# An MLP with its up and down projections apart, f kept on DRAM, and Strassen's seven block products in most of the down projection (Trainium2, one core)

## The chip, the core and the metric

The kernel runs on one core of a Trainium2 chip. The metric is the device time of one execution in microseconds, as the median of several runs; before the change it is 2465.88 us. A profile of one execution shows where the time goes on TensorE (PE, with its weight loads as PEld), VectorE (DVE), ScalarE (ACT), GpSimd (POOL) and the queue that issues DMAs (SP).

## What is computed

A trunk of two layers on 1024 tokens of width 1024 with 16 learned tokens ahead of them: differential attention, then a gated short convolution, each followed by an MLP with a squared ReLU. All in float32. The MLP is what the change concerns:

```python
def _sqrelu_mlp(h, w_up, w_down):          # w_up [1024, 4096], w_down [4096, 1024]
    a = jax.nn.relu(jnp.einsum('bld,df->blf', h, w_up))
    return jnp.einsum('blf,fd->bld', a * a, w_down)
```

The MLP's input is an RMSNorm of the residual stream, and its output is normed and added to the stream; layer 0's goes on into the convolution's three projections, layer 1's is the kernel's output.

## The kernel before

Activations stay transposed, channels on the 128 partitions and tokens along the columns. Every float32 product runs as three float32r passes: an operand is split into a part rounded to float32r (hi) and the remainder (lo), and hi·hi, hi·lo and lo·hi add up in PSUM (`product`, L166 to 174). Layer 0 works on T1 = 1026 columns (two learned tokens are still needed by the convolution), cut in three of 342; layer 1 on 1024, cut in two of 512.

Weights come as tiles of 128 x 1024 in the order of their use (`load_weights`, L122): SP loads 512 KB (L132), ScalarE casts hi (L143), VectorE subtracts lo (L144). Two pools, `wp` and `wx`, give two raw tiles and four pairs of hi and lo, so the next tiles are loaded and split ahead.

`mlp` (L406) goes through the 4096 f channels in 8 blocks of 4 tiles of 128. For a block it first does the up projection of each f tile over the 8 chunks of the input (24 matmuls per column chunk): VectorE takes the ReLU times the norm's scale out of PSUM (L424), ScalarE squares (L425), VectorE casts and subtracts (L426, L427) into `fh` and `fl`, which stay in SBUF. Then four weight tiles of the down projection, each for 256 output channels: 4 f tiles by 3 passes, 12 matmuls per half and column chunk. The result is copied into the accumulator `acc` in the first block (L450) and added to it in the others (L452). In the last block the squares for the following norm are summed on GpSimd (L198), and the norm is made where the columns are whole: `norm_step` (L354) in layer 0, `last_step` (L338) at the end of layer 1.

```python
for group in [[0, 1, 2, 3]] if last else [[0], [1], [2], [3]]:
...
    product(ps, w, lambda k, c: fh[k][:, c[0] : c[0] + c[1]],
            lambda k, c: fl[k][:, c[0] : c[0] + c[1]], half * FB * P, range(FB), cols)
```

PSUM has eight banks, of which seven go round for products. The order of the instructions on each engine is found by a scheduler from the program's dependences, except in stretches that fix it by hand (the attention's TensorE, the end of layer 1). `later`, `spent` and `settle` (L318 to 336) put the steps of a norm where enough products have been traced to cover them. After layer 0's MLP the convolution starts with a joint stage of four weight tiles, c and u of two channel groups (L552).

Of the kernel before, what the change touches and what calls it, by code (L numbers as in the profile page):

```python
# [23 lines left out]
P = 128  # L24
# [5 lines left out]
LEAD = META - 2  # L30
# [4 lines left out]
NB = FF // (FB * P)  # L35
# [3 lines left out]
CONV_ORDER = [0, 1, 3, 4, 2, 5] + list(range(6, 3 * KC))  # L39
REACH = T0 - P  # L40
BANKS = {"mm": 2, "s": 3, "t": 2, "o": 1}
E_BUFS = 3
EARLY = 3  # rows of the output projection begun within the attention
# the startup: steps of products between others, parts of the sums of squares, columns, banks of the first products
# [7 lines left out]
# engines and lags as the attention's order takes them  # L52
# [10 lines left out]
# the last layer's end: columns, squares summed on the tensor engine, and where each step goes  # L63
# [16 lines left out]
def trunk(ctx: ExitStack, tc: tile.TileContext, xt, wall, gains, lam_p, subln, convw, out):  # L80
# [7 lines left out]
    psp = ctx.enter_context(tc.tile_pool(name="psp", bufs=2, space=PSUM))  # L88
    drp = ctx.enter_context(tc.tile_pool(name="drp", bufs=1, space=DRAM))

    # one table serves every function used
# [15 lines left out]

    def big_tile(half, name, dtype=F32):
        return big.tile([P, 4, T0], dtype, tag=f"big{half}", name=f"{name}{half}")

    def late_tile(dtype):
        t = cst.tile([P, 2 * EARLY * P], dtype, tag="late", name="late" if dtype == F32R else "rs")
        return t if dtype == F32 else t.rearrange("p (a b) -> p a b", a=2)
# [8 lines left out]
    def load_weights(eng=None, raw=None, spare=None, early=None):  # L122
        """The next tile; gives what splits it. Of an early one, the last chunk's columns go to tiles of their own."""
# [29 lines left out]
    count = [0]  # L153

    def bank(tag, name):
        count[0] += 1
        return psp.tile([P, 512], F32, tag=tag, name=f"{name}_{count[0]}", bufs=BANKS[tag])

    ROUND = ["mm", "s", "t", "mm", "s", "t", "mm"]
    turn = [0]  # L160

    def any_bank(name):
        turn[0] += 1
        return bank(ROUND[turn[0] % len(ROUND)], name)

    def product(ps, w, hi, lo, w0, ks, cols):  # L166
        """ps += W^T x over the contraction chunks ks; W's chunk k starts at column w0 + k * P."""
        wh, wl = w
        n, last = 0, 3 * len(ks) - 1
        for j, k in enumerate(ks):  # L170
            a, b = w0 + j * P, w0 + (j + 1) * P
            for lhs, rhs in ((wh, hi), (wh, lo), (wl, hi)):
                nc.tensor.matmul(ps, lhs[:, a:b], rhs(k, cols), start=n == 0, stop=n == last)  # L173
                n += 1

    def rsqrt_mean(tp, ps, dst, n, dim):
        """dst = (-ps / dim + eps) ** -0.5, with a Newton step on what the tables give."""
# [7 lines left out]
    def total(sss, n):  # L185
        """minus the sum over the partitions of all of sss"""
        ps = bank("o", "sum")[:, :n]
# [12 lines left out]
    # ======== layer 0: differential attention ========  # L200
# [3 lines left out]
    HL = hpool.tile([P, KC, T0], F32R, name="HL")  # L204
# [8 lines left out]
    with pool("att") as att:  # L213
        with pool("xin", side="right") as xin, tc.manual_schedule(engines={ET.PE, ET.Activation, ET.DVE, ET.Pool}):
# [30 lines left out]
            def raw(z, cs):  # L245
                """not scaled yet by the norm: what these columns' products give is"""
# [60 lines left out]
    sp = ctx.enter_context(pool("sp", 3))  # L307
    wpools.append(ctx.enter_context(pool("wx", 2)))
# [4 lines left out]
    # ======== the rest ========  # L313
    # A step that closes a norm waits on other engines, so it is traced where that many us of products lie before it.
# [18 lines left out]
    def settle(step, cols):  # L333
        """what cols of the coming stage need of the steps up to this one"""
# [3 lines left out]
    def last_step(tp, m, sss, cols, res, res_out):  # L338
        """res_out <- res + rmsnorm(m) where m is gained already"""
# [14 lines left out]
    def norm_step(tp, layer, which, m, mss, cols, res_in, res_out, nxt, H, L, ssn, wait):  # L354
        """m <- res + rmsnorm(m), stored; then m * gain split into H and L, and its scale into ssn."""
# [6 lines left out]
        def add():  # L362
            rs = mss[:, s]
            rsqrt_mean(tp, total([rs], n), rs, n, D)
            for c4 in range(0, KC, 4):
                cs = slice(c4, c4 + 4)
                st = tp.tile([P, 4, n], F32, tag="st", name=f"st_{count[0]}_{c4}", bufs=2)
                nc.sync.dma_start(st, res_in(cs, s))
                for c in range(c4, c4 + 4):
                    mc, hc, gn = row(m, c, s), row(H, c, s), gain(nxt[0], nxt[1], c)  # L370
                    nc.vector.scalar_tensor_tensor(mc, mc, gain(layer, which, c), rs, ALU.mult, ALU.mult)
                    nc.vector.tensor_add(mc, mc, st[:, c - c4])
                    nc.scalar.activation(hc, mc, AF.Copy, scale=gn)
                    nc.vector.scalar_tensor_tensor(row(L, c, s), mc, gn, hc.bitcast(F32), ALU.mult, ALU.subtract)  # L374
                    add_square(tp, ssn[:, s], mc, c == 0, n, tag="sqn")
                nc.sync.dma_start(res_out(cs, s), m[c4 // 4][:, :, s])
# [29 lines left out]
    def mlp(tp, fp, hi, lo, rs, target, head, chunks, tail, after, final=False):  # L406
        """after(chunk, sum, its squares' sum) when a chunk is whole; target() once what came before is closed."""
        for b in range(NB):
            fh, fl = [], []
            for i in range(FB):  # L410
                fh.append(fp.tile([P, T1], F32R, tag="fh", name=f"fh_{b}_{i}", bufs=FB))
                fl.append(fp.tile([P, T1], F32R, tag="fl", name=f"fl_{b}_{i}", bufs=FB))
            for group in [list(range(FB))] if b == 0 else [[i] for i in range(FB)]:
                ws = [weights() for _ in group]
                for cols in head if b == 0 else chunks:
                    c0, n = cols
                    s = slice(c0, c0 + n)
                    for i, w in zip(group, ws):
                        ps = any_bank("up")[:, :n]
                        settle(0, cols)  # L420
                        product(ps, w, hi, lo, 0, range(KC), cols)
                        settle(1, cols)
                        r = fp.tile([P, n], F32, tag="r", name=f"r_{count[0]}", bufs=2)
                        nc.vector.scalar_tensor_tensor(r, ps, 0.0, rs[:, s], ALU.max, ALU.mult)  # L424
                        nc.scalar.activation(r, r, AF.Square)  # L425
                        nc.vector.tensor_copy(fh[i][:, s], r)  # L426
                        nc.vector.tensor_sub(fl[i][:, s], r, fh[i][:, s].bitcast(F32))  # L427
                        spent(3 * KC, n)
            last = b == NB - 1
            sqs, steps, scales, manual = [], [], [], ExitStack()  # L430
            if final and last:
                for c in range(0, KC, 2):
                    nc.sync.dma_start(YL[:, c : c + 2].bitcast(F32), res_dram[2][:, c : c + 2, :SEQ])
            if b == 0:
                acc, ass = target()
            for group in [[0, 1, 2, 3]] if last else [[0], [1], [2], [3]]:
                ws = [weights() for _ in group]
                for cols in tail if last else chunks:
                    if final and last and cols == tail[-1]:
                        manual.enter_context(tc.manual_schedule(engines=MANUAL))  # L440
                    c0, n = cols
                    s = slice(c0, c0 + n)
                    for gi, w in zip(group, ws):
                        for half in range(2):
                            mi = 2 * gi + half
                            ps, am = any_bank("dn")[:, :n], row(acc, mi, s)
                            product(ps, w, lambda k, c: fh[k][:, c[0] : c[0] + c[1]],
                                    lambda k, c: fl[k][:, c[0] : c[0] + c[1]], half * FB * P, range(FB), cols)
                            if b == 0:
                                nc.scalar.copy(am, ps)  # L450
                            else:
                                nc.vector.tensor_add(am, am, ps)  # L452
# [657 lines left out]
```

## Time and profile before

| what | value |
| --- | --- |
| median of 3 runs | 2465.88 us (2465.83 to 2465.95) |
| span of the profiled execution | 2461.8 us |
| around the span | 4.1 us |
| TensorE busy | 2405.5 us, 98% |
| VectorE, ScalarE, GpSimd busy | 1293.5, 868.1, 287.8 us |
| moved by DMA | 164.17 MB, 67 GB/s |

The span runs from the first to the last instruction. Busy shares are means over the whole span; the rows further down are read by stage.

### The profile page before, as it was taken

To read this page: it belongs to the slowest core of one execution; us is meant where nothing else is said; L and a number is where in the kernel's file an instruction comes from. 1 tells how busy PE (TensorE), PEld (TensorE's weight loads), DVE (VectorE), ACT (ScalarE), POOL (GpSimd) and SP (SyncE) were. 2 spreads that over 40 slices of the span, in tenths; PEclk is the share of its full clock that TensorE was granted. 3 is DMA by queue.
4 is the path that set the end of the run, shared out by engine and by line. 5 is a ranking of instruction groups with operands and counts; after the bars stand their busy time and mean duration, and the time that the engine had idled before them with its cause. 6 is when DMAs were issued, how large, how long until landed. Compare 5 with 4: busy or idle time off the path is not lost.

```text
span 2461.8 us, 34993 instructions
## 1 busy us (share of the span) xinstructions
PE 2405.5 (98%) x14186; PEld 2261.5 (92%) x14186; DVE 1293.5 (53%) x2559; ACT 868.1 (35%) x1725; POOL 287.8 (12%) x246
## 2 busy tenths in 40 slices
PE   8999999999999999999999999999999999999997
PEld 7899999999899999999999999999888888888887
DVE  7887777755823443443446934424823433433346
ACT  7777777655521111111114422224521111111125
POOL 3211211105200000000004200004200000000006
PEclk9999999999999999999999999999999999999998
DMA  4212222533511111111113411123411111111122
GB/s 133 65 53 61 61 62 68 137 106 92 140 52 44 50 45 44 52 44 52 44 52 81 117 47 43 52 66 79 122 52 43 52 43 52 43 52 43 52 70 102
DMA packets 77553, 164.17 MB, mean 67 GB/s; under 512 B 7248, under 2 KB 51664, under 8 KB 77392
## 3 DMA queue, kind: packets, MB, share of 16 engines
q1 hardware_dynamic: 77392, 161.94, 22.6%
q8 instruction: 111, 1.82, 0.3%
q14 instruction: 50, 0.41, 0.1%
HBM read 129.25 MB, written 24.15 MB: 62 GB/s over the span
## 4 chain that ended last, share of the span: by engine, by line
PE 83%; DVE 10%; DMA 2%; ACT 2%; issue 1%; SPq 0%; DVEq 0%; ACTq 0%
PE dn L173 27%; PE up L173 27%; PE mo L173 4%; PE bg L173 4%; PE ug L173 3%; PE cg L173 3%; PE po L1022 2%; DVE HL L374 1%; PE tr L983 1%; PE s L936 1%; PE s L937 1%; DMA w_raw<-in_wall 1%; PE v L689 1%; PE v L690 1%; PE v L691 1%
## 5 line engine op out<-in xcount | busy, mean ns | idle before, releaser
L143 ACT CAST w_hi<-w_raw 128x1024 fp32r<-128x1024 f32 (+2 forms) x191 | 199.2, 1043 | 792.7 <-PE dn L173 495.2
L173 PE MATMUL dn<-fh,w_hi 128*128 128x342 f32 (+2 forms) x1344 | 458.7, 341 | 0.5 <-DVE acc L452 0.5
L173 PE MATMUL dn<-fl,w_hi 128*128 128x342 f32 (+2 forms) x1344 | 458.1, 341 | 0.0
L173 PE MATMUL dn<-fh,w_lo 128*128 128x342 f32 (+2 forms) x1344 | 457.0, 340 | 0.0
L144 DVE TENSOR_TENSOR w_lo<-w_raw,w_hi 128x1024 fp32r<-128x1024 f32 (+1 forms) x167 | 206.3, 1235 | 228.3 <-ACT w_hi L143 228.2
L173 PEld LDWEIGHTS dn<-fh,w_hi 128*128 128x128 f32 x1344 | 253.1, 188 | 20.8 <-DVE acc L452 0.7
L173 PEld LDWEIGHTS dn<-fl,w_hi 128*128 128x128 f32 x1344 | 253.2, 188 | 19.6
L173 PEld LDWEIGHTS dn<-fh,w_lo 128*128 128x128 f32 x1344 | 252.9, 188 | 19.8
L173 PE MATMUL up<-HL,w_hi 128*128 128x342 f32 x768 | 246.1, 321 | 2.0 <-DVE HL L374 2.0
L173 PE MATMUL up<-HH,w_hi 128*128 128x342 f32 x768 | 245.4, 320 | 0.0
L173 PE MATMUL up<-HH,w_lo 128*128 128x342 f32 x768 | 244.9, 319 | 0.0
L424 DVE SCALAR_TENSOR_TENSOR r<-up,ssn 128x342 f32<-128x342 f32 (+2 forms) x164 | 93.8, 574 | 286.6 <-PE up L173 286.1
L425 ACT ACTIVATE r<-r 128x342 f32<-128x342 f32 (+2 forms) x164 | 87.8, 538 | 350.7 <-DVE r L424 350.5
L173 PE MATMUL up<-YL,w_hi 128*128 128x512 f32 (+2 forms) x544 | 209.1, 385 | 0.6 <-DVE YL L374 0.6
L198 POOL TENSOR_TENSOR ass<-ass,sq 128x256 f32<-128x256 f32 (+1 forms) x47 | 44.4, 944 | 1330.0 <-ACT sq L197 1329.6
L452 DVE TENSOR_TENSOR acc<-acc,dn 128x512 f32<-128x512 f32 (+1 forms) x128 | 78.7, 619 | 175.7 <-PE dn L173 175.5
L173 PEld LDWEIGHTS up<-HL,w_hi 128*128 128x128 f32 x768 | 144.7, 188 | 3.3 <-DVE HL L374 2.8
L173 PEld LDWEIGHTS up<-HH,w_lo 128*128 128x128 f32 x768 | 144.6, 188 | 0.3
L173 PEld LDWEIGHTS up<-HH,w_hi 128*128 128x128 f32 x768 | 144.8, 189 | 0.1
L173 PEld LDWEIGHTS up<-YL,w_hi 128*128 128x128 f32 x544 | 102.7, 189 | 21.4 <-DVE YL L374 1.2
L946 ACT ACTIVATE E<-E,mn 16x16 f32<-16x16 f32 (+5 forms) x144 | 105.2, 731 | 21.8 <-DVE mn L941 21.5
L173 PE MATMUL up<-YHa,w_hi 128*128 128x512 f32 (+2 forms) x272 | 104.3, 384 | 2.4 <-DVE r L424 2.4
(296 smaller groups left out, 5370.6 us busy)
## 6 DMA issues: line engine op xcount, KB each, us to landing
w_raw<-in_wall SPq DMA_DIRECT2D x189, 512.0 KB, 3.5
st<-res_dram SPq DMA_DIRECT2D x10, 684.0 KB, 9.6
st<-in_xt SPq DMA_DIRECT2D x6, 684.0 KB, 8.6
YL<-res_dram SPq DMA_DIRECT2D x4, 1024.0 KB, 9.4
HL<-on_dram SPq DMA_DIRECT2D x3, 1026.0 KB, 8.4
HH<-on_dram SPq DMA_DIRECT2D x3, 1026.0 KB, 11.0
out<-acc SPq DMA_DIRECT2D x12, 256.0 KB, 2.2
klb<-klb SPq DMA_DIRECT2D x32, 87.0 KB, 2.1
```

Of the source, the lines that this page charges most:

```text
L143: nc.scalar.copy(hi_part, raw[:, cols])
L144: (eng or nc.vector).tensor_sub(lo_part, raw[:, cols], hi_part.bitcast(F32))
L173: nc.tensor.matmul(ps, lhs[:, a:b], rhs(k, cols), start=n == 0, stop=n == last)
L198: (eng or nc.gpsimd).tensor_add(ss, ss, sq)
L374: nc.vector.scalar_tensor_tensor(row(L, c, s), mc, gn, hc.bitcast(F32), ALU.mult, ALU.subtract)
L424: nc.vector.scalar_tensor_tensor(r, ps, 0.0, rs[:, s], ALU.max, ALU.mult)
L425: nc.scalar.activation(r, r, AF.Square)
L452: nc.vector.tensor_add(am, am, ps)
L689: nc.tensor.matmul(ps, wh[:, a], self.HH[:, k, s], start=k == 0, stop=False)
L690: nc.tensor.matmul(ps, wh[:, a], self.HL[:, k, s], start=False, stop=False)
L946: nc.scalar.activation(e[:rows, :ext], e[:rows, :ext], AF.Exp, scale=-1.0, bias=mn, accum_out=H["sums"][:rows, c : c + 1])
L1022: nc.tensor.matmul(po[:, a0:ncols], v[:, j], a[:, j, a0:ncols], start=j == 0 and z == 0, stop=j == nch - 1 and z == 2)
```

## The change

The MLP becomes a function of five stages (`mlp`, lines 613 to 660 of the changed kernel). The up projection of all 32 f tiles runs first, and f goes to DRAM. Then the down projection runs over it.

1. The first four f tiles are made as before and written to `plain_dram`.
2. Twelve times, `up_pair` makes two f tiles, halves their tokens (H = 514 columns in layer 0, where T1 becomes 1028, and 512 in layer 1), and so has a 2 x 2 block of f. From it VectorE makes the seven operands of Strassen's scheme (in Winograd's form) in the free slots of an accumulator's half. ScalarE casts them, VectorE subtracts, and the seven pairs of hi and lo, 3.68 MB, go to `seven_dram` from one tile `stage`.
3. The last four f tiles are made as before, and `down_plain` multiplies them at once, beginning the accumulator. Meanwhile the operands of the first block come back into the tiles that held the MLP's input.
4. `Sevens.run` takes six blocks of four f tiles. A weight tile q (2 x 2 blocks of weights, 24 tiles per layer) needs four sums of weight blocks, made by GpSimd (`combine`), and splits of 512, 1024 and 256 columns. Seven block products of 6 matmuls each (12 in layer 0, where 514 columns lie across two PSUM banks, 258 and 256) replace eight. Their sums run up in PSUM, and each step's state is added to a quarter of the accumulator (VectorE, line 588). Operands of the next block are loaded slot by slot behind the products, into two sets of tiles.
5. The first four f tiles come back from `plain_dram`, and `down_plain` ends the accumulator, with the squares and the norm as before.

Around it: one weight pool in the MLP in place of two, PSUM laid out anew for each stage (`psum_stage`), residual tiles of `norm_step` of two channels in place of four, and a convolution that starts with three weight tiles (c, u of group 0 and c of group 1), the u of group 1 after b of group 0.

The core of the diff (`down_plain` is the old loop over the halves of a weight tile, `split` a cast and a subtraction as in `load_weights`):

```diff
-LEAD = META - 2
+PRE = 4
+LEAD = META - PRE
 T1 = T0 - LEAD
...
+    def up_pair(fp, hi, lo, rs, H, t, chunks, stage, spool):
+        v = flat(t)[:, : 8 * H].rearrange("p (a b) -> p a b", a=8)
+        for e in range(2):
+            w = weights()
+            for cols in chunks:
+                c0, n = cols
+                r = up_product(fp, w, hi, lo, rs, cols)
+                for z in range(2):
+                    a, b = max(c0, z * H), min(c0 + n, (z + 1) * H)
+                    if a < b:
+                        nc.scalar.activation(v[:, SLOT[e, z], a - z * H : b - z * H], r[:, a - c0 : b - c0], AF.Square)
...
+        nc.vector.tensor_sub(v[:, 3], v[:, 7], v[:, 0])
+        nc.vector.tensor_sub(v[:, 2], v[:, 5], v[:, 3])
+        nc.vector.tensor_sub(v[:, 4], v[:, 5], v[:, 7])
+        nc.vector.tensor_sub(v[:, 6], v[:, 1], v[:, 2])
...
+        for a, b in ((0, 4), (4, 7)):
+            nc.scalar.copy(sv[:, a:b, 0], v[:, a:b])
+            nc.vector.tensor_sub(sv[:, a:b, 1], v[:, a:b], sv[:, a:b, 0].bitcast(F32))
+            nc.sync.dma_start(spool[:, a:b], sv[:, a:b].bitcast(F32))
...
+        def combine(self, q):
...
+            nc.gpsimd.tensor_add(s1, a21, a22)
+            nc.gpsimd.tensor_sub(s2, s1, a11)
+            nc.gpsimd.tensor_sub(s3, a11, a21)
+            nc.gpsimd.tensor_sub(s4, a12, s2)
...
+        def product(self, ps, slot, q, first):
...
+            for off, c, n in ([(254, 0, 258), (512, 258, 256)] if H > 512 else [(0, 0, H)]):
+                k = 0
+                for j in range(2):
+                    a = w0 + j * P
+                    for lhs, t in ((wh, 0), (wh, 1), (wl, 0)):
+                        nc.tensor.matmul(ps[:, off : off + n], lhs[:, a : a + P], F[j][slot][:, t, c : c + n],
+                                         start=first and k == 0, stop=k == 5, skip_group_check=not first)
...
+            def step(slot, q):
...
+                chain = {0: "a", 1: "c", 2: "a", 3: "b", 4: "a", 5: "b", 6: "a"}[slot]
+                first = slot in (0, 1, 3)
...
+                nc.vector.tensor_add(am, am, got)
+                if q % 4 == 3:
+                    b = q // 4
+                    if b + 2 < NW:
+                        self.load(b + 2, slot)
...
+                for q in range(n + 1):
+                    if q + 2 < n:
+                        self.fetch(q + 2)
+                    if q + 1 < n:
+                        self.combine(q + 1)
+                    step(4, q - 1)
+                    step(5, q - 1)
+                    step(1, q)
+                    step(6, q - 1)
+                    if q + 1 < n:
+                        self.settle(q + 1)
+                    step(2, q)
+                    step(3, q)
+                    step(0, q + 1)
...
+    def mlp(layer, hi, lo, rs, H, two, base, base_plain, head, chunks, opened, psum_of, reopen):
...
+        st = stage()
+        up_plain(fp, hi, lo, rs, W, st, [list(range(FB))], head, True)
+        for i, f in enumerate(quarters(st, W)):
+            nc.sync.dma_start(plain[:, i * FB : (i + 1) * FB], f.bitcast(F32))
...
+        for j in range(2 * NW):
+            up_pair(fp, hi, lo, rs, H, two(j % 2, f"f{layer}_{j}"), chunks, stage(), spool[j])
+        st = stage()
+        up_plain(fp, hi, lo, rs, W, st, [[i] for i in range(FB)], chunks)
+        seven = Sevens(wd, H, base, spool)
+        for slot in range(7):
+            seven.load(0, slot)
+        acc = [two(i, f"acc{layer}") for i in range(2)]
+        for g in range(FB):
+            down_plain(acc, *quarters(st, W), [g], chunks, lambda mi, cols, am, ps: nc.scalar.copy(am, ps))
+        seven.fetch(0)
+        seven.combine(0)
+        seven.settle(0)
+        seven.fetch(1)
+        ff.close()
+        psum_stage(*psum_of)
...
+            seven.run(acc, [[sevens(t, H)[:, k] for k in range(7)] for t in fx], after_base)
...
-        conv_in([(0, "c"), (0, "u"), (1, "c"), (1, "u")])
+    conv_in([(0, "c"), (0, "u"), (1, "c")])
```

What the change moves shows in the order of SP, which issues the DMAs. Before, where layer 0's MLP begins, the norm's last transfers (`st`, `res_dram`) are followed by weight tiles alone:

```order
L368 DMA st_0_13413<-res_dram_77 128x4x342
L376 DMA res_dram_77<-m0b 128x4x342
L368 DMA st_4_13442<-res_dram_77 128x4x342
L132 DMA w_raw_8073<-in_wall 128x1024
L132 DMA w_raw_8351<-in_wall 128x1024
L132 DMA w_raw_8253<-in_wall 128x1024
```

After, in layer 0's up pairs, the two writes of a pair's `stage` (four slots and three) stand between the weight tiles, which are those of pairs to come:

```order
L494 DMA seven_dram_79<-stage_634_9943 128x4112
L494 DMA seven_dram_79<-stage_634_9943 128x3084
L138 DMA w_raw_10427<-in_wall 128x1024
L138 DMA w_raw_10523<-in_wall 128x1024
L494 DMA seven_dram_79<-stage_640_10137 128x4112
L494 DMA seven_dram_79<-stage_640_10137 128x3084
L138 DMA w_raw_10619<-in_wall 128x1024
```

So a weight tile is now queued behind 3.68 MB of writes. Further on, at the plain down block of layer 0, the last of 14 loads of a block's operands (into `HH` and `HL`, the MLP's input until then), then that block's third and fourth weight tile, the first three of the seven products, and the loads for the second block (`fx`):

```order
L521 DMA HH<-seven_dram_79 128x1028
L521 DMA HL<-seven_dram_79 128x1028
L138 DMA w_raw_10911<-in_wall 128x1024
L138 DMA w_raw_11001<-in_wall 128x1024
L528 DMA w_raw_11091<-in_wall 128x1024
L528 DMA w_raw_11156<-in_wall 128x1024
L528 DMA w_raw_11230<-in_wall 128x1024
L521 DMA fx_0_11124<-seven_dram_79 128x1028
```

The first two weight tiles of the plain block stand ahead of the 14 loads; these two stand behind them.

On VectorE, before, in a down block of layer 0, an add per product, and a weight split between them:

```order
L452 TENSOR_TENSOR acc0a<-acc0a,dn_9521 128x342
L452 TENSOR_TENSOR acc0a<-acc0a,dn_9535 128x342
L452 TENSOR_TENSOR acc0a<-acc0a,dn_9549 128x342
L452 TENSOR_TENSOR acc0a<-acc0a,dn_9563 128x342
L144 TENSOR_TENSOR w_lo_9858<-w_raw_9855,w_hi_9857 128x1024
L452 TENSOR_TENSOR acc0a<-acc0a,dn_9583 128x342
L452 TENSOR_TENSOR acc0a<-acc0a,dn_9597 128x342
```

After, for one weight tile of the seven products (`pa`, `pb`, `pc` are the running sums in PSUM; `s_`, `a_`, `d_` the splits of the sums of weights, of the first two blocks and of the last):

```order
L588 TENSOR_TENSOR acc0b<-acc0b,pa_12374 128x514
L588 TENSOR_TENSOR acc0b<-acc0b,pb_12479 128x514
L536 TENSOR_TENSOR s_lo_720_12580<-s_tmp_719_12515,s_hi_720_12579 128x1024
L588 TENSOR_TENSOR acc0a<-acc0a,pc_12550 128x514
L536 TENSOR_TENSOR a_lo_12512<-w_raw_12509,a_hi_12511 128x512
L588 TENSOR_TENSOR acc0b<-acc0b,pa_12374 128x514
L536 TENSOR_TENSOR d_lo_720_12584<-w_raw_12390,d_hi_720_12583 128x256
L588 TENSOR_TENSOR acc0a<-acc0a,pa_12495 128x514
L588 TENSOR_TENSOR acc0a<-acc0a,pb_12600 128x514
```

Before, a weight tile in layer 0 has six adds of 342 columns and one split of 1024; now it has seven adds of 514 and three splits, of 512, 1024 and 256.

## Rows read from the trace of the kernel before

**Rows 1.** The page, parts 1 and 2: busy time by engine, and 40 slices.

```profile
PE 2405.5 (98%) x14186; PEld 2261.5 (92%) x14186; DVE 1293.5 (53%) x2559; ACT 868.1 (35%) x1725; POOL 287.8 (12%) x246
PE   8999999999999999999999999999999999999997
PEclk9999999999999999999999999999999999999998
GB/s 133 65 53 61 61 62 68 137 106 92 140 52 44 50 45 44 52 44 52 44 52 81 117 47 43 52 66 79 122 52 43 52 43 52 43 52 43 52 70 102
```

**Rows 2.** The chain of waits: start, length, engine, product, line, matmuls.

```profile
709.63 45.31 PE up L173 x288
754.94 45.28 PE dn L173 x288
2307.47 44.48 PE dn L173 x192
2351.95 44.63 PE up L173 x192
2396.58 18.39 PE dn L173 x156
```

**Rows 3.** Windows: start and end, length, busy time of each engine.

```profile
core 0: us, PE busy (x) PEld busy (x) DVE busy (x) ACT busy (x) POOL busy (x), PEclk, DMA share, GB/s
709.70:755.00 45.30, 45.30 (x290) 45.30 (x289) 19.73 (x38) 9.63 (x17) 0.00 (x0) 1.00 0.15 47
2396.58:2414.97 18.39, 18.39 (x158) 18.39 (x157) 7.82 (x16) 12.39 (x26) 6.97 (x10) 1.00 0.44 175
1319.00:1399.80 80.80, 77.32 (x459) 73.65 (x458) 77.24 (x129) 45.51 (x96) 38.84 (x35) 0.98 0.51 120
```

**Rows 4.** Groups by line and shape: 1770 to 2396, the last one 664 to 1319.

```profile
line engine op names shapes xcount | busy us, mean ns | idle before us <-releasers
L144 DVE TENSOR_TENSOR w_lo<-w_raw,w_hi 128x1024 fp32r<-128x1024 f32 x58 | 71.1, 1225 | 45.9 <-ACT w_hi L143 45.9
L452 DVE TENSOR_TENSOR acc<-acc,dn 128x512 f32<-128x512 f32 x96 | 66.0, 687 | 161.6 <-PE dn L173 161.6
L143 ACT CAST w_hi<-w_raw 128x1024 fp32r<-128x1024 f32 x58 | 61.0, 1052 | 357.4 <-PE dn L173 245.9 <-PE up L173 106.9 <-DMA w_raw<-in_wall 4.6
L424 DVE SCALAR_TENSOR_TENSOR r<-up,ssn 128x512 f32<-128x512 f32 x55 | 38.0, 692 | 156.2 <-PE up L173 156.2
L425 ACT ACTIVATE r<-r 128x512 f32<-128x512 f32 x55 | 34.8, 632 | 141.9 <-DVE r L424 141.9
L424 DVE SCALAR_TENSOR_TENSOR r<-up,ssn 128x342 f32<-128x342 f32 x86 | 44.3, 515 | 127.0 <-PE up L173 127.0
```

**Rows 5.** Windows where DMA is densest; columns as in rows 3.

```profile
6.00:20.00 14.00, 12.82 (x60) 11.82 (x61) 11.40 (x18) 11.88 (x25) 2.64 (x1) 1.00 1.04 372
2394.00:2408.00 14.00, 14.00 (x111) 13.51 (x110) 5.77 (x12) 8.03 (x16) 4.10 (x6) 1.00 0.75 293
1380.00:1387.00 7.00, 6.81 (x43) 6.53 (x43) 7.00 (x11) 5.61 (x14) 6.37 (x6) 1.00 0.74 199
```

**Rows 6.** DMA issues: KB each, median us from issue to landing.

```profile
w_raw<-in_wall SPq DMA_DIRECT2D x189, 512.0 KB, 3.5
```

**Rows 7.** GpSimd's adds (2396 to 2444), line 374, and the accumulator (min/median/max).

```profile
L198 POOL TENSOR_TENSOR ass<-ass,sq 128x256 f32<-128x256 f32 x25 | 20.4, 815 | 653.6 <-ACT sq L197 653.2
L374 DVE SCALAR_TENSOR_TENSOR HL<-m0a,g,HH x12: 566/1160/1296, 593.4 to 647.7; 128x342 fp32r<-128x342 f32 x12
L374 DVE SCALAR_TENSOR_TENSOR HL<-acc0a,g,HH x12: 562/1190/1251, 1333.7 to 1387.1; 128x342 fp32r<-128x342 f32 x12
L452 DVE TENSOR_TENSOR acc<-acc,dn x128: 407/686/689, 1865.0 to 2445.1; 128x512 f32<-128x512 f32 x96, 128x256 f32<-128x256 f32 x32
```

More of the change, by code (lines that the diff above doesn't have):

```diff
@@ L34 @@
 FB = 4
-NB = FF // (FB * P)
+NF = FF // P
+NW = NF // FB - 2
 EPS = 1e-6
@@ L185, in total @@
     def total(sss, n):
-        ps = bank("o", "sum")[:, :n]
+        ps = bank(psum["sums"], "sum")[:, :n]
         for i, ss in enumerate(sss):
@@ new lines, in up_plain @@
+    def up_plain(fp, hi, lo, rs, W, stage, groups, chunks, boundary=False):
+        fh, fl = quarters(stage, W)
+        for group in groups:
+            ws = [weights() for _ in group]
+            for cols in chunks:
+                s = slice(cols[0], cols[0] + cols[1])
+                for i, w in zip(group, ws):
+                    r = up_product(fp, w, hi, lo, rs, cols, boundary)
+                    nc.scalar.activation(r, r, AF.Square)
+                    nc.vector.tensor_copy(fh[:, i, s], r)
+                    nc.vector.tensor_sub(fl[:, i, s], r, fh[:, i, s].bitcast(F32))
+                    spent(3 * KC, cols[1])
@@ new lines, in down_plain @@
+    def down_plain(acc, fh, fl, group, chunks, done):
+        ws = [weights() for _ in group]
+        for cols in chunks:
+            c0, n = cols
+            s = slice(c0, c0 + n)
+            for gi, w in zip(group, ws):
+                for half in range(2):
+                    mi = 2 * gi + half
+                    ps = any_bank("dn")[:, :n]
+                    product(ps, w, lambda k, c: fh[:, k, c[0] : c[0] + c[1]], lambda k, c: fl[:, k, c[0] : c[0] + c[1]],
+                            half * FB * P, range(FB), cols)
+                    done(mi, cols, row(acc, mi, s), ps)
+                    spent(3 * FB, n)
@@ new lines, in trunk @@
+    h = SEQ // 2
+    base = [[v for t, n in zip(YH, (4, 3)) for v in [sevens(t, h, n)[:, k] for k in range(n)]],
+            [sevens(HL, h)[:, k] for k in range(7)]]
+    acc, last = mlp(1, yh, yl, ssn, h, two1, base, last_quarters(*YH, SEQ), fine, cut1, third,
+                    ("psp3", {"a": 3, "b": 2, "c": 2, "o": 1}, 512, ["a", "b", "c", "a", "b", "c", "a"], "o"), lambda: None)
+    mp = ctx.enter_context(pool("mlp1b", 2))
+    ass = stat("ass1")
+    ends = [sum(TAIL[:i]) for i in range(len(TAIL))]
@@ new lines, in trunk, with done1 @@
+    tail = list(zip(ends, TAIL))
+    for c in range(0, KC, 2):
+        nc.sync.dma_start(YL[:, c : c + 2].bitcast(F32), res_dram[2][:, c : c + 2, :SEQ])
+    res = YL.bitcast(F32)
+    sqs, steps, scales, manual = [], [], [], ExitStack()
+    def done1(mi, cols, am, ps):
+        c0, n = cols
+        s, ending = slice(c0, c0 + n), cols == tail[-1]
+        if ending and mi == 0:
+            manual.enter_context(tc.manual_schedule(engines=MANUAL))
+        nc.vector.tensor_add(am, am, ps)
+        direct = DIRECT[ending]
+        if mi >= KC - direct:
+            if mi == KC - direct:
+                sqs.clear()
+            sq = mp.tile([P, n], F32, tag="sqn", name=f"sqn_{c0}_{mi}", bufs=2)
+            nc.scalar.activation(sq, am, AF.Square)
+            sqs.append(sq)
+        else:
+            add_square(mp, ass[:, s], am, mi == 0, n)
+        scale = partial(nc.scalar.activation, am, am, AF.Copy, scale=gain(1, 3, mi))
+        if ending and mi >= KC - LATE:
+            scales.append(scale)
+        else:
+            scale()
+        if mi == DEFER:
+            steps[:] = [part for step in steps for part in step()]
+        for _ in range(FINISH[mi]):
+            if steps:
+                steps.pop(0)()
+        if mi == KC - 1:
+            steps.append(partial(last_step, mp, acc, [ass[:, s], *sqs], cols, res, lambda c, s: out[:, c, s]))
+            sqs.clear()
@@ L590 @@
+    down_plain(acc, *last, list(range(FB)), tail, done1)
+    for step in steps:
+        parts = step()
+        for scale in scales:
+            scale()
+        for part in parts:
+            part()
+    manual.close()
+    settle(1, (0, SEQ))
 class Attention:
```

414 lines of the change are left out of this document (230 added, 184 removed).

## The prediction, on record before the changed kernel ran

> **What bounds the kernel now.** I read the page first: TensorE is busy 2405.5 us, 98% of the span, in every slice and at full clock, while DMA moves little [rows 1]. What ends the time is therefore TensorE's own work, and a change gains what it takes from that work, less the idle time it brings. The chain of waits says the same for the stretches that the change rewrites: through both MLPs it is one product stage after the other with no gap, 45.3 us per up or down block of 288 matmuls in layer 0, 44.5 us per down block of 192 in layer 1 [rows 2]. The windows show what stands beside: in an up block of layer 0 VectorE is busy for 19.7 of 45.3 us, ScalarE for 9.6, GpSimd idle, DMA at a share of 0.15 [rows 3]. So there is room on the other engines for a scheme that spends adds and DMA to save products. Where the room ends is the second question: at the join from a norm to the next stage (1319 to 1399.8 us) VectorE is busy 77.24 of 80.8 us, and TensorE loses 3.5 there.
>
> The profiled execution took 2461.8 us of span; the median of the runs is 2465.88, so 4.1 us lie around the span. I take the sum off the median.
>
> **What the change saves.** A matmul of 342 columns takes 45.28/288 = 0.1572 us, one of 512 takes 44.48/192 = 0.2317, one of 256 takes 18.39/156 = 0.1179 [rows 2], with the weight-load row full in that last window and still not setting the pace [rows 3]. One weight tile of a down projection is 72 matmuls of 342 columns in layer 0, 11.32 us. Seven block products are 7 x 12 = 84 of 258 or 256 columns; at 0.1183 (the 256 row scaled to 257 columns) that is 9.94 us. Gain 1.38, times 24 tiles: 33.1 us. In layer 1 a tile is 48 matmuls of 512 columns; seven products of 6 leave 42, so 24 x 6 x 0.2317 = 33.4 us. **Together 66.5 us.** This needs no estimate but one: that 258 columns which begin at column 254 of one PSUM bank, and 256 in the next, run at the rate of the 256 row.
>
> **What it costs.**
> 1. Two more token columns in layer 0 and the convolution's input: 768 full-width products of the up projection, 192 of the output projection and 576 of the convolution, 1536 x 2 x 0.46 ns = 1.4 us.
> 2. *The up pairs.* A pair of f tiles takes 22.6 us of TensorE (half of 45.3). VectorE: six relu steps 3.1, two weight splits 2.45, four differences of 514 columns 2.8 and the split of 3598 columns 4.3 (by the 1225 ns row of 1024) = 12.7; ScalarE about 9.4 [rows 4]. Both are hidden. The stage tile exists once, so the next pair's cast waits for both writes: cast of four slots 2.1 + split 2.45 + fixed time of a DMA 2.1 + 3.68 MB at the write rate W. The fixed time is 3.5 us for 512 KB less 1.4 at 372 GB/s [rows 5, 6]. At 372 GB/s the chain is 16.6 us and hidden; it reaches 22.6 at W = 231. The two rows that bracket W are the read at 372 GB/s and share 1.04, and the stretch with two writes of the residual, 199 at share 0.74 [rows 5]. I take it as above 231, since 199 at three quarters of the engines is 269 at all of them: cost 0. The other end is rival B. Weights are queued behind a pair's writes on SP, but two tiles ahead of their use, and with both the DMA engines move 4.73 MB in 22.6 us, 209 GB/s.
> 3. *The first plain block.* Its writes must end before the first pair casts, and VectorE may stand blocked at the split while relu steps queue behind it: 1.5 us a layer, 3 (0 to 5 a layer).
> 4. *Third weight tile of the plain down block.* The order puts it on SP behind 14 loads of 526 KB, which fill the tiles that the up products have just read and so cannot start before. 7.37 MB at 372 GB/s = 19.8, its own 3.5, cast 1.05, split 1.2 [rows 4 to 6]: 25.6 us, against the 22.6 that two tiles cover. 3.0 a layer, 6 (0 if the order's first tiles last longer; 8.3 a layer at the 293 GB/s of the YL loads).
> 5. *Changes of stage.* Into the seven products the first cast and the bank change, 1.1; out of them the first plain weights' cast and split, 2.3: 3.4 a layer, 6.8 (0 to 7 a layer).
> 6. *The seven products.* Per weight tile VectorE has seven adds of 514 columns at 0.69, and splits of 1024, 512 and 256 columns, 1.23 + 0.69 + 0.42: 7.2 us of 9.94 [rows 4]. GpSimd has four adds of 256 columns, 3.3 us at 0.82 [rows 7]. The loads of a block are 7.37 + 2.1 MB in 39.8 us, 238 GB/s, under both read rows. A block accumulator is read by VectorE and added to two products later, 2.8 us, against 0.69 and at most one 1.23 split ahead. I put 0.1 us a tile for what does not fit, 48 tiles, 5 us (0 to 24).
> 7. *Layer 0's norm into the convolution.* That join is the fullest for VectorE [rows 3], and the third weight tile of the convolution is now started before one u stage less: one part of 11.3 us less cover, but that part's VectorE work leaves as well. 4 us (0 to 11.3).
>
> Sum of costs 1.4 + 0 + 3 + 6 + 6.8 + 5 + 4 = 26.2, so the gain is 40.3 and **the forecast 2465.9 - 40.3 = 2426 us**. With all the waits at nothing it is 2465.9 - 65.1 = 2401; with terms 4, 5 and 7 at their upper ends (16.6, 14, 11.3) 2451.
>
> **Rivals.**
> A. *All the joins hide.* Scheduling has put first whatever is ready; then 2401 to 2404. For it: the old joins cost TensorE only 3.5 us in 80 [rows 3]. Against it: term 4 is an order on one queue that nothing can pass. Chance 0.08.
> B. *Slow writes (slower than before).* If the stage's writes go at 199 GB/s, the chain is 2.1 + 2.45 + 2.1 + 18.5 = 25.1 us against 22.6 (22.3 in layer 1). ScalarE's cast then blocks ScalarE's squares and VectorE's split blocks the relu steps, PSUM fills up and TensorE waits: 11 x (2.5 + 2.8) = 59 us, 2485. It decides from 231 GB/s down; at 209 the whole gain is gone. For it: the only row of writes on their own is that of 199 GB/s [rows 5]. Against it: that stretch had engines to spare. Chance 0.13.
> C. *VectorE and GpSimd hold each other up.* VectorE's splits read two tensors in SBUF, as line 374 does: 562 ns at least, but a median of 1160 to 1190 in the norms, where GpSimd works, while the accumulator's add, whose second operand is in PSUM, stays at 686 with a longest of 689 [rows 4, 7]. In the seven products GpSimd's 3.3 us per tile stand beside these splits. If VectorE loses all of that, it has 7.2 + 3.3 = 10.5 us of work in 9.94: 0.5 more per tile than the forecast's cover allows, 24 us in place of the 5 of term 6: 2445; at 1.0 per tile, 2469. Against it: GpSimd is idle two thirds of the time, and nothing says that its adds meet the splits rather than the accumulators' adds. The Trainium skill (SBUF — State Buffer, Who interferes with whom) states as a rule that a VectorE instruction with two SBUF inputs contends with a GpSimd instruction that reads SBUF, and one of them blocks fully; the trace agrees in kind, 562 against 1160 to 1190 ns. Chance 0.14.
> D. *Split products miss the row rate.* If the products across two banks in layer 0 cost as much as what they replace, that layer gains nothing: 2426 + 33 = 2459. No row shows such a product. Chance 0.05.
>
> The forecast keeps 0.60.
>
> **How the numbers follow.** The range 2402 to 2470 holds the forecast with its upper bounds (2451), C and D; B is left out above (0.13) and the lower half of A below. A measurement of this kernel can tell about 0.2%, 5 us, from no change. Faster by more than that: the forecast, A, most of C and half of D, 0.82; within it, C's far end and the rest of D, 0.05; slower, B, 0.13.
>
> **What would show it.** Right: TensorE's busy time down by about 65 us to 2340, and its idle time in the two MLPs up by some 20 to 30. A chain of waits with groups of seven products (84 or 42 matmuls) at 9.94 and 9.73 us per tile; a gap of about 3 us before the third tile of each plain down block; up pairs at 22.6 us without gaps, and the stage's writes landing within 12 us. B shows as idle TensorE between up pairs with VectorE's split waiting for the stage's write. C shows as splits of 1024 columns near 2 us in the seven products and TensorE waiting for an accumulator's add. The forecast is wrong at its root if TensorE's busy time has not dropped by 60 us, or if idle time appears in the up pairs.

## The result, and the profile after

The changed kernel takes 2450.26 us (median of 4, 2446.46 to 2453.48) against 2465.91 for the kernel before beside it: a ratio of 0.9934, with a 95% interval of 0.992 to 0.9948. It is faster by 15.7 us. The forecast was faster by 40, to 2426 us; the time lies in the range given, but the gain is under half of what was forecast.

The page of the changed kernel, parts 1 and 2, and the chain of waits (start, length, what):

```profile
PE 2358.9 (96%) x14330; PEld 2215.5 (90%) x14330; DVE 1483.7 (61%) x2655; ACT 996.2 (41%) x1893; POOL 433.1 (18%) x438
...
PEclk9999999999999999999998899999999999999999
```

```profile
666.78 325.30 PE up L187 x2069
992.08 45.08 PE dn L187 x288
...
1053.21 2.88 PE pa L565 x24
...
1063.25 2.88 PE pa L565 x24
...
1785.18 318.56 PE up L187 x1395
2103.73 44.79 PE dn L187 x192
...
2154.36 2.80 PE pa L565 x12
...
2164.11 2.80 PE pa L565 x12
```

Beside [rows 1, 2], TensorE's busy time fell by 46.6 us, not by 65, and the granted clock has two slices of 8 at layer 0's last norm, where before there was none. In the chain the MLPs look as forecast: the up projections of layer 0 run 325 us in one piece, twelve pairs with their writes in it; the plain down block runs 45.08 us in one piece; a weight tile of the seven products takes 1063.25 - 1053.21 = 10.04 us in layer 0 and 2164.11 - 2154.36 = 9.75 in layer 1 (expected 9.94 and 9.73).

The windows of the changed kernel, columns as in [rows 3]:

```profile
675.10:992.10 317.00, 317.00 (x2018) 316.83 (x2017) 162.46 (x211) 109.00 (x162) 0.00 (x0) 1.00 0.55 204
1043.20:1274.10 230.90, 230.90 (x1934) 230.90 (x1934) 159.37 (x226) 44.71 (x65) 68.50 (x84) 1.00 0.60 222
1274.10:1288.70 14.60, 11.40 (x77) 10.34 (x75) 6.79 (x9) 3.43 (x4) 0.00 (x0) 1.00 0.45 160
1305.00:1366.50 61.50, 33.35 (x165) 29.39 (x165) 44.48 (x73) 29.68 (x60) 31.69 (x28) 0.73 0.39 126
```

In the up pairs and in the seven products TensorE is busy for all of 317.0 and 230.9 us. The loss stands in one place above all: from 1305 to 1366.5 us, in layer 0's last norm, where TensorE works for 33 of 61.5 us, at a clock of 0.73.

So I divided both profiles at the same events. Where the seven products of the changed kernel end (1278.4 and 2383.5 us), the kernel before ends its last up tile. Lengths in us, of the profiled executions (that of the changed kernel is the longest of its four, 2453.48 us, span 2451.7):

| stretch | before | after | difference |
| --- | --- | --- | --- |
| start to the end of layer 0's output projection | 582.2 | 587.0 | +4.8 |
| to the end of the first four up tiles (norm 1) | 82.1 | 88.1 | +6.0 |
| to the end of the last up tile or of the seven products (MLP 0) | 634.1 | 603.3 | -30.8 |
| to the start of layer 1's output projection (last down block, norm 2, convolution) | 327.7 | 360.9 | +33.2 |
| to the end of the first four up tiles (norm 3) | 146.7 | 152.0 | +5.3 |
| to the end of the last up tile or of the seven products (MLP 1) | 623.7 | 592.2 | -31.5 |
| to the end | 65.2 | 68.2 | +3.0 |

The two MLPs give 62.3 us, near the 66.5 of the product count. Three joins take 44.5 of it back; the first line is scatter (580.8 to 587.0 over two profiles of the changed kernel). Of the runs below, one execution of the kernel called best took 3832 us at a granted clock of 0.56, and its ratio leaves that one out.

### The profile page after: what moved, and what is told of

It reads as the page before. It is cut to its first block, busy times and chain, and to the rows that moved or that the text cites. A ratio compares the mean times of both kernels' runs of the same rounds, so it can differ in the third digit from the quotient of the medians.

```text
span 2451.7 us, 36477 instructions
## 1 busy us (share of the span) xinstructions
PE 2358.9 (96%) x14330; PEld 2215.5 (90%) x14330; DVE 1483.7 (61%) x2655; ACT 996.2 (41%) x1893; POOL 433.1 (18%) x438
## 4 chain that ended last, share of the span: by engine, by line
PE 81%; DVE 10%; ACT 4%; issue 2%; DMA 2%; POOL 1%; SPq 0%; DVEq 0%; POOLq 0%; ACTq 0%
PE up L187 27%; PE pa L565 11%; PE pb L565 6%; PE dn L187 5%; PE mo L187 4%; PE cg L187 4%; PE ug L187 4%; PE bg L187 4%; PE pc L565 3%; PE po L1272 2%; DVE HL L392 1%; PE tr L1233 1%; PE s L1186 1%; DMA w_raw<-in_wall 1%; PE s L1187 1%
## 5 line engine op out<-in xcount | busy, mean ns | idle before, releaser
L187 PE MATMUL up<-HL,w_hi 128*128 128x344 f32 (+3 forms) x1312 | 455.9, 348 | 6.4 <-DVE HL L392 6.2
L187 PEld LDWEIGHTS up<-HL,w_hi 128*128 128x128 f32 x1312 | 248.5, 189 | 30.1 <-DVE HL L392 9.4
L187 PE MATMUL up<-HH,w_hi 128*128 128x344 f32 (+1 forms) x768 | 246.7, 323 | 7.1 <-ACT HH L391 4.7
L456 DVE SCALAR_TENSOR_TENSOR r<-up,ssn 128x344 f32<-128x344 f32 (+3 forms) x164 | 92.9, 571 | 254.9 <-PE up L187 254.7
L187 PE MATMUL up<-HH,w_lo 128*128 128x344 f32 (+1 forms) x768 | 245.7, 321 | 0.0
L187 PE MATMUL up<-YHa,w_lo 128*128 128x512 f32 (+2 forms) x272 | 104.7, 385 | 0.0
L187 PE MATMUL up<-YHb,w_lo 128*128 128x512 f32 (+2 forms) x272 | 103.8, 382 | 0.0
L187 PE MATMUL up<-YHb,w_hi 128*128 128x512 f32 (+2 forms) x272 | 103.4, 380 | 0.0
L187 PE MATMUL mo<-HL,w_hi 128*128 128x342 f32 (+2 forms) x312 | 99.6, 319 | 0.0
L588 DVE TENSOR_TENSOR acc<-acc,pa 128x512 f32<-128x512 f32 x96 | 65.9, 686 | 32.8 <-PE pa L565 31.2
```

Of the source, the lines that this page charges most:

```text
L456: nc.vector.scalar_tensor_tensor(r, ps, 0.0, rs[:, c0 : c0 + n], ALU.max, ALU.mult)
L588: nc.vector.tensor_add(am, am, got)
```

## The experiments

Three sets of four kernels; each set has its own runs of the kernel before, with medians of 2470.3, 2469.7 and 2469.4 us. Ratios are to these, with 95% intervals; they are the recorded ones, and differ from the quotient of two medians by up to 0.001. For the reading of single stretches each profile was divided at four events of its chain (the end of layer 0's output projection and of its last up product, the start of layer 1's output projection, the end of its last up product); lengths in us:

| kernel | ratio | norm 1 and ups 0 | downs 0, norm 2, convolution | projection 1, norm 3, ups 1 | to the end |
| --- | --- | --- | --- | --- | --- |
| changed, again | 0.9917 | 405.1 | 646.1 | 463.2 | 348.0 |
| psum | 0.9874 | 407.0 | 633.5 | 463.5 | 348.2 |
| oldnorm1 | 0.9863 | 399.3 | 646.1 | 457.7 | 348.2 |
| sqn1 | 0.9869 | 398.7 | 645.8 | 457.9 | 348.2 |
| sqnall | 0.9831 | 400.3 | 639.3 | 458.7 | 348.0 |
| psum_sqn | 0.9803 | 406.9 | 619.4 | 464.4 | 351.7 |
| psum_exit | 0.9886 | 405.3 | 636.1 | 463.7 | 353.1 |
| best | 0.9777 | 398.9 | 621.9 | 456.3 | 353.5 |
| final | 0.9752 | 399.2 | 619.0 | 457.2 | 348.3 |

**again.** The changed kernel, as the reference of the set.

> The changed kernel again, beside the others of this set, as their reference. Expected 2447 to 2453 us, and the gap between the seven products of layer 0 and the convolution's bg products near 126 us, as in the first profile (1276.9 to 1402.5). If that gap moves by more than 5 us from one run to the next, the single profiles can't be compared to that accuracy.

2447.87 us, 0.9917 (0.9904 to 0.9931). The stretches agree with the first profile's to 1.3 us, but for the first one, ahead of the MLP.

**psum.**

```diff
+    psum_stage("psp2", BANKS, 512, ROUND, "o")
     down_plain(acc, *last, list(range(FB)), cut0, done0)
-    psum_stage("psp2", BANKS, 512, ROUND, "o")
```

> PSUM is laid out anew (seven banks for products) ahead of layer 0's last plain down block rather than behind it. Theory 1 (four wide PSUM tiles: TensorE's products wait for VectorE's adds, which stand behind the norm): the stretch from the last of the seven products to the convolution's bg products shrinks by 15 us or more, total 2430 to 2437 us. Theory 2 (squares: the norm's and the accumulator's squares share two tiles, and GpSimd and ScalarE take them in the wrong order): that stretch stays within 4 us of 126, total 2446 to 2454 us, and TensorE's sum still waits some 13 us for GpSimd's add. Theory 3 (one weight tile less to work on in the convolution's first stage): also no change here.

2437.99 us, 0.9874 (0.9859 to 0.9889). The stretch with layer 0's last norm is 12.6 us shorter, nothing else moves by more than 2. In the changed kernel TensorE's products (`dn`) wait in that join for VectorE's adds of the accumulator, 6.9 us in two waits; here that wait is gone. Theory 1 holds for a part: four tiles of 1024 columns, each used for 344, are too few where VectorE's adds stand behind a norm. But from 1305 to 1366.5 us TensorE still stood idle for 12.1, so it is not the whole.

**four.** The kernel before with `LEAD = META - 4`, and the convolution's offsets to fit.

> The kernel before, with four of the learned tokens kept in place of two (1028 columns), and nothing else. If the 4.8 us that the changed kernel loses ahead of the first MLP come from the wider columns (transfers and stat tiles of 260 columns in the attention), this kernel takes 2470 to 2474 us and its output projection ends near 587 us; if they come from the pools laid out anew, it takes 2467 to 2468 us (1.4 us by the column count) and the projection ends near 582.5.

2463.03 us, 0.9972 (0.9963 to 0.9981): neither. Two more columns cost nothing; in this set they even ran 7 us shorter, for which I have no cause (its profile's span, 2461.1, is within 1 us of that of [rows 1]'s kernel). The projection ended at 583.1. The 4.8 us of the first line are not the columns.

**oldnorm1 and sqn1.** In `norm_step` ahead of the MLPs, all of the old step, or one word of it:

```diff
-                        add_square(tp, ssn[:, s], mc, c == 0, n)
+                        add_square(tp, ssn[:, s], mc, c == 0, n, tag="sqn" if which == 1 else "sq")
```

> The changed kernel, with the old norm step ahead of both MLPs: residual tiles of four channels in two buffers, and the norm's squares in tiles of their own. If this edit makes the joins into the MLPs 5.9 and 5.3 us longer, the time falls by 8 to 11 us, to 2439 to 2442 us. If it is the order of the weights' casts on ScalarE ahead of the norm, or the single stage tile behind the first relu steps, the time stays within 3 us of the changed kernel's.

> The changed kernel, with the norm's squares in tiles of their own ahead of the two MLPs, and nothing else. Theory: of the old norm step it is the squares' tiles that gave back 11 us in the joins (and some 14 in all); then this takes the ratio to the kernel before from 0.992 to 0.986 to 0.988. Rival: it is the residual's tiles (two channels in place of four); then the ratio stays at 0.991 to 0.993.

oldnorm1 2434.02 us, 0.9863 (0.985 to 0.9877); sqn1 2437.14 us, 0.9869 (0.9853 to 0.9886). Both joins fall by 5 to 6 us, the same with the one word as with the whole old step. It is the squares' tiles, not the residual's.

**three.** The kernel before, with the convolution's start from the change: `conv_in([(0, "c"), (0, "u"), (1, "c")])`, and u1 behind b0.

> The kernel before, with the convolution's start of the changed kernel alone: three weight tiles (c0, u0, c1) worked on together in place of four, u1 behind b0. Theory 3 (that stage covers layer 0's last norm, and a fourth less of it costs what the prediction's term 7 put at 4 us, or more): 4 to 11 us slower than the kernel before in the same set. Theory 1 and 2 alone: within 2 us.

2470.55 us, 1.0006 (0.9997 to 1.0015). Theory 3 falls: a weight tile less to cover the norm costs nothing here.

**psum_exit.** On top of psum, the last plain block's weights from raw tiles that come free early:

```diff
+        forced.extend([(wx, wx), (wp, wp), (wx, wx), (wx, wp)])
...
+        first, src = forced.pop(0) if forced else (src, src)
...
-            raw = src.tile([P, 1024], F32, tag="w_raw", name=f"w_raw{i}", bufs=1)
+            raw = first.tile([P, 1024], F32, tag="w_raw", name=f"w_raw{i}", bufs=1)
```

> On top of seven banks for the last plain block: its four weight tiles are loaded into raw tiles of two pools that come free early (the first and third behind the seven products' raw tile, the second in wp, the fourth behind the third), so that no load stands on SP behind a split that waits for the last of the seven products. Theory: the gap of 11.9 us in layer 0 and 8.7 in layer 1 behind the seven products is that queue; then it falls to about 3.5 us in each, the split of the first tile, and the time is 11 to 14 us under the version with seven banks alone (2424 to 2427 us if the kernel before stands at 2470, in ratio 0.982). Rival (the loads are late because transfers of the last operands fill the DMA engines): the gap stays over 7 us.

2442.54 us, 0.9886 (0.9872 to 0.9899), no faster than psum (two stretches are 2.6 and 4.9 us longer). The theory was a misreading. The chain passes through the cast, the split and a load there, but TensorE works beside them on the tiles that it has: the window above shows 11.40 us of products in those 14.60. TensorE lost 3.2 us, not 11.9, and 1.0 in layer 1, not 8.7. Why the two stretches are longer wasn't looked into. A chain of waits says what the end hung on, not that TensorE was idle.

**psum_sqn.** On top of psum, the tag as in sqn1, but in layer 0's last norm (`which == 3`), with two residual tiles in place of three there.

> On top of seven banks for the last plain block: the squares of layer 0's last norm have tiles of their own again (paid for with two residual tiles in place of three). Theory 2: ScalarE's squares for the accumulator then no longer wait for GpSimd's adds of the norm's squares; the stretch from the seven products to the convolution's bg products falls by 6 to 10 us below the version with seven banks, to a ratio near 0.984. If the shared tiles were only bystanders: within 2 us of it, a ratio of 0.987.

2421.74 us, 0.9803 (0.979 to 0.9817). The stretch falls by another 14.1 us, more than expected. (Its last stretch is 3.5 us longer than psum's; the profile is that of the longest of its five executions.) Theory 2 holds. GpSimd's timeline shows how; first the changed kernel (start, length, adds, and idle time before them with its releaser):

```profile
1300.93 0.93 POOL L212 TENSOR_TENSOR ass<-ass,sq 128x344 f32<-128x344 f32 x1 [0.97 <-ACT sq L211]
1315.39 2.33 POOL L212 TENSOR_TENSOR rs<-rs,sq 128x344 f32<-128x344 f32 x2 [13.53 <-ACT sq L211]
1319.06 2.34 POOL L212 TENSOR_TENSOR rs<-rs,sq 128x344 f32<-128x344 f32 x2 [1.34 <-ACT sq L211]
1321.74 4.31 POOL L212 TENSOR_TENSOR rs<-rs,sq 128x344 f32<-128x344 f32 x3 [0.35 <-ACT sq L211]
1326.02 8.26 POOL L212 TENSOR_TENSOR ass<-ass,sq 128x344 f32<-128x344 f32 x7
```

and TensorE's, where the accumulator's second column chunk is multiplied, and its squares' sum is wanted:

```profile
1318.10 0.48 PE L187 MATMUL dn<-HL,w_hi 128*128 128x344 f32 x2
...
1325.76 0.58 PE L187 MATMUL dn<-HL,w_hi 128*128 128x340 f32 x2 [1.38 <-DVE acc0a L695]
...
1334.34 1.51 PE L203 MATMUL sum<-ass,minus 128*128 128x344 f32 x2 [6.44 <-POOL ass L212]
```

The second chunk's products are done by 1318.6. Its seven adds of squares (`ass`) start at 1326.0, behind all seven of the first chunk's norm (`rs`), which wait for VectorE's steps one after the other. Two tiles go round among both kinds of squares in the order of the program text; there, one chunk's norm stands ahead of the next chunk's accumulator squares. So the early ones wait for the late ones, the sum for them, the next chunk's norm for the sum, and the convolution for that norm. With tiles of their own (the version called final, below, whose seven products end 11 us earlier) the two kinds alternate, and the second chunk's are through by 1307 (`128x344`):

```profile
1302.34 2.20 POOL L212 TENSOR_TENSOR rs<-rs,sq 128x344 f32<-128x344 f32 x2 [0.29 <-ACT sq L211]
1304.50 2.38 POOL L212 TENSOR_TENSOR ass<-ass,sq 128x344 f32<-128x344 f32 x2
1306.83 1.22 POOL L212 TENSOR_TENSOR rs<-rs,sq 128x344 f32<-128x344 f32 x1
1308.01 1.19 POOL L212 TENSOR_TENSOR ass<-ass,sq 128x340 f32<-128x340 f32 x1
1309.16 1.20 POOL L212 TENSOR_TENSOR rs<-rs,sq 128x344 f32<-128x344 f32 x1
```

**sqnall.** The changed kernel with the tag apart in all three norms, PSUM as changed.

> The changed kernel, with the squares of all three norms in tiles of their own, and PSUM as the change has it (four wide tiles in layer 0's last plain block). If squares and PSUM cost separately, 11 + 14 us less than the changed kernel: a ratio of 0.981 to 0.983. If the squares in layer 0's last norm only matter once there are seven banks, about 11 us less: 0.986 to 0.988.

2427.35 us, 0.9831 (0.9817 to 0.9846). In layer 0's last norm the tag gives 6.9 us with four wide tiles and 14.1 with seven banks; banks alone give 12.6, both 27. There each repair is worth more beside the other.

**shared.** The other way round, the kernel before with the one word taken out (L375, the only edit):

```diff
-                    add_square(tp, ssn[:, s], mc, c == 0, n, tag="sqn")
+                    add_square(tp, ssn[:, s], mc, c == 0, n)
```

> The kernel before, with the one word changed that makes the norm's squares share the two tiles of the accumulator's squares. If that edit alone costs the joins what it cost in the changed kernel (6 + 5 in front of the MLPs, 14 in layer 0's last norm), this is 20 to 28 us slower than the kernel before, a ratio of 1.008 to 1.011. If it needs the rest of the change, under 5 us, 1.000 to 1.002.

2499.41 us, 1.0122 (1.0107 to 1.0137): 30 us slower. Between the same events the three joins grow by 10.0, 13.8 and 12.5 us. GpSimd shows the same picture, seven adds of `rs` in one piece ahead of those of the next chunk:

```profile
1324.51 0.92 POOL L198 TENSOR_TENSOR ass<-ass,sq 128x342 f32<-128x342 f32 x1 [0.96 <-ACT sq L197]
1339.11 9.22 POOL L198 TENSOR_TENSOR rs<-rs,sq 128x342 f32<-128x342 f32 x7 [13.68 <-ACT sq L197]
1348.29 6.42 POOL L198 TENSOR_TENSOR ass<-ass,sq 128x342 f32<-128x342 f32 x5
```

So this one word, with no part of the new MLP, makes the stall.

**best and final.** All repairs, and those that paid (psum, oldnorm1, and the tag in layer 0's last norm with two residual tiles there).

> All repairs together: seven banks for the last plain block, the old norm step ahead of the MLPs, separate squares in layer 0's last norm, weights of the last block loaded early. If the losses are separate, the gains add up: 10 (banks) + 14 (norm step) + 11 to 14 (exit) + 0 to 8 (squares) off the changed kernel's 2447.9 us, 2404 to 2413 us, a ratio of 0.973 to 0.977. If they hide one another, 2420 us or more.

> The changed kernel with the three repairs that paid (seven banks in layer 0's last plain block, the old norm step ahead of the MLPs, separate squares in layer 0's last norm) and without the loads for the last block: 2421.7 - 11 = 2410 us, a ratio of 0.975 to 0.977, below the version with all repairs (0.9777) if the early loads cost the 2.6 and 4.9 us by which their stages were longer.

best 2415.01 us, 0.9777 (0.9764 to 0.9791); final 2408.16 us, 0.9752 (0.9738 to 0.9767). Leaving the early weight loads out is worth 7 us: with them the second and last stretches are 2.9 and 5.2 us longer. The final version beats both kernels, by 61 us the one before. Its page and two windows, the last norm with the convolution's start in the second:

```profile
PE 2341.6 (97%) x14330; PEld 2202.2 (92%) x14330; DVE 1487.4 (62%) x2655; ACT 994.7 (41%) x1893; POOL 443.0 (18%) x438
...
PEclk9999999999999999999999999999999999999998
```

```profile
663.50:980.70 317.20, 317.20 (x2020) 317.20 (x2019) 161.69 (x210) 108.63 (x161) 0.00 (x0) 1.00 0.55 203
1265.00:1372.00 107.00, 97.16 (x592) 93.36 (x592) 87.82 (x137) 54.32 (x110) 45.01 (x42) 0.98 0.39 123
```

TensorE's busy time is now 63.9 us under that of [rows 1], with the same 14330 instructions as the changed kernel, and its idle time in that join is 9.8 us of 107.

## Why the prediction was right and wrong

**What it saves: right.** 66.5 us were put on the products; the two MLP stretches are 62.3 us shorter with their costs in them, and TensorE's busy time in the final version is down by 63.9. In the changed kernel itself it is down by 46.6, under the 60 that the prediction gave as the sign of being wrong at its root: the products are as counted, but at the joins some of them ran at a lower clock (last section). One reading was too broad: "in every slice and at full clock" doesn't hold for the two ends of [rows 1]. The products that lie across two banks run at the row rate (10.04 against 9.94 us a tile), so rival D falls.

**Term 2, the up pairs: right.** TensorE waits for nothing there. The writes go at a rate near the upper of the two rows that bracketed them; KB each and us from issue to landing in the changed kernel:

```profile
seven_dram<-stage SPq DMA_DIRECT2D x12, 2056.0 KB, 6.4
...
seven_dram<-stage SPq DMA_DIRECT2D x12, 1542.0 KB, 9.3
```

2.1 MB in 6.4 us is at least 329 GB/s, latency included, where 231 decided. Rival B falls, and with it the 199 GB/s of [rows 5], which was the rate of a stretch that had little to write (1.40 MB in 7 us).

**Terms 4 to 6: too dear.** The third weight tile of the plain block (6 us) cost nothing: 288 and 192 products in one piece. In layer 0 the 14 loads began at 988.7 us, 3.4 ahead of the block, where the prediction's sum let them begin with it, and the third tile landed at 1010.9, in time for products at 1014.5. Changes of stage (6.8) cost 3.2 and 1.0 us of idle time behind the seven products and nothing ahead of them. The seven products (5) cost 24 x 0.10 and 24 x 0.02 = 2.9.

**Rival C falls, but its contention is there.** Groups by line in the seven products of layer 0, changed kernel:

```profile
L588 DVE TENSOR_TENSOR acc0b<-acc0b,pa 128x514 f32<-128x514 f32 x46 | 31.7, 689 | 16.4 <-PE pa L565 16.1
...
L536 DVE TENSOR_TENSOR s_lo<-s_tmp,s_hi 128x1024 fp32r<-128x1024 f32 x22 | 27.0, 1225 | 6.9 <-ACT s_hi L535 6.9
...
L536 DVE TENSOR_TENSOR a_lo<-w_raw,a_hi 128x512 fp32r<-128x512 f32 x20 | 15.9, 796 | 6.4 <-ACT a_hi L535 6.3
L543 POOL TENSOR_TENSOR s_tmp<-w_raw 128x256 f32<-128x256 f32 x21 | 15.7, 748 | 141.8 <-DVE s_lo L536 105.5 <-DVE acc0a L588 22.2 <-DMA w_raw<-in_wall 14.1
...
L536 DVE TENSOR_TENSOR d_lo<-w_raw,d_hi 128x256 fp32r<-128x256 f32 x22 | 11.0, 500 | 0.0
```

The split of 1024 columns takes the 1225 ns of [rows 4]. GpSimd's first sum waits for it (105.5 us of idle time), since `s_tmp` exists once: these two cannot meet. The smaller splits and GpSimd's adds do meet. Splits of 512 columns take 692 to 1220 ns, 796 in the mean where term 6 had 690; those of 256 columns take 500 where it had 420; and GpSimd's adds take from 729 to 1197. That is 0.2 us a tile on VectorE, which is busy for 159.4 of the 230.9 us of that window, so TensorE waits for none of it. The Trainium skill (SBUF — State Buffer, Who interferes with whom) states that a VectorE instruction with two SBUF inputs contends with a GpSimd instruction that reads SBUF. The trace agrees, in these splits and in the norms, where line 374's successor (392) takes between 558 and 1252 ns.

**Terms 3 and 7, the joins: the step that failed.** They were put at 3 and 4 us. Norms 1 and 3 cost 6.0 and 5.3, and norm 2 33.2, of which 3.2 belong to term 5: 41.3 us in place of 7. What term 3 priced, the writes behind the first plain block, cost nothing (TensorE is busy for all of the 317.0 us that follow); the loss stands ahead of them, in the norms, for which there was no term. Two edits did most of it, and the prediction priced neither. The first is the word that `norm_step` lost, its squares' own tag. The text read that function's edit as residual tiles of another size and stopped there, though the line stands in the full diff; the runs give it 11 us in norms 1 and 3 and 7 to 14 in norm 2. The second is PSUM: term 5 counted its change ahead of the seven products, but not that layer 0's last plain block then runs on the four wide tiles, in the one block whose adds stand behind a norm: 12.6 us, and 27 with the tag. What term 7 did price, the convolution's start with three tiles, costs nothing (three: 1.0006). And the forecast had named this join as the fullest for VectorE [rows 3], which is where a lost buffer shows. That the time still lies in the range, and just under the 2451 of the upper bounds, is luck: those bounds held terms 4, 5 and 7 at 41.9 us, of which 4.2 came.

In the final version the stretch of norm 2, from the end of the seven products (1267.0) to layer 1's output projection (1599.7), is 332.7 us: 5.0 of the 33.2 us are left. What makes them wasn't tried.

## What to carry to other kernels

When a change replaces the steady part of a kernel, count its products for the gain, but go through every helper that runs at the joins, line by line: a tag shared by two kinds of temporaries fixes their order, and the one that is ready first waits for the one that is late. PSUM banks are cover as much as space; where a stage's adds queue behind a norm, their number sets how far TensorE gets. And before mending a gap that the chain of waits shows, look at the busy time in that window.

## What was not expected of the hardware

A stall on TensorE was paid twice here. In the changed kernel the granted clock fell to half behind the idle time of the last norm, and products then ran at half speed; windows of 5 us, columns as in [rows 3]:

```profile
1325.00:1330.00 5.00, 2.14 (x12) 1.85 (x12) 4.99 (x8) 2.14 (x4) 4.84 (x4) 1.00 0.33 105
1340.00:1345.00 5.00, 0.00 (x0) 0.00 (x0) 5.00 (x12) 3.10 (x8) 0.04 (x1) 0.50 0.07 6
1345.00:1350.00 5.00, 3.77 (x12) 3.33 (x12) 5.00 (x6) 2.91 (x7) 4.02 (x4) 0.50 0.98 337
```

At a granted 0.50, the lower of its two levels (1.2 of 2.4 GHz), twelve products of 340 columns took 3.77 us, 0.31 each, against 0.157 per product of 342 columns at the upper one. It fell behind idle time: from 1327.9 to 1345.2 us TensorE ran only four short sums. The changed kernel's TensorE is busy 17.3 us longer than the final version's (2358.9 and 2341.6) for the same number of instructions, at a mean clock of 0.983 against 0.995. The prediction had priced idle time, and not the slow time behind it.
